# Sixteen 512-byte stores of zeros to the last tile's rows, sent on ScalarE's queue with the first load

## The chip, the core and the metric

The kernel runs on one NeuronCore of a Trainium2 chip. The metric is device time in microseconds (us) of one execution; the span that the profile shows is some 1.7 us shorter.

## The reference

```python
def reference(x, factor):            # x: 16 x 3 x 512 x 512 float32, factor 1.5
    mean = np.mean(x, axis=(2, 3), keepdims=True)
    return np.clip(mean + factor * (x - mean), 0, 1).astype(np.float32)
```

50.33 MB come in and 50.33 MB go out. There are 48 images; a tile of 128 partitions by 8192 elements (4.19 MB) holds four of them, so there are 12 tiles.

## The kernel before

Six tile buffers are loaded ahead on SyncE's queue (q1 in the profile). For each tile, VectorE sums one half of the columns and ScalarE the other, TensorE turns the sums into a bias, ScalarE applies scale, bias and Relu, and VectorE the upper bound. The tile's store goes out on ScalarE's queue (q10), and a buffer is loaded again when its store has landed.

```python
P = 128; ROW = 8192; BUFS = 6; CHUNK = 2048
...
    def load(t):
        xt = xpool.tile([P, ROW], f32, name="xt")
        nc.sync.dma_start(out=xt, in_=dram(x_f, t))
        tiles[t] = xt
...
    def store(t):
        nc.scalar.dma_start(out=dram(out_f, t), in_=tiles.pop(t))

    with tc.manual_schedule():
        for t in range(min(BUFS, n_tiles)):
            load(t)
        for t in range(n_tiles):
            compute(t)
            store(t)
            if t + BUFS < n_tiles:
                load(t + BUFS)
```

## Time and profile before

| | before |
|---|---|
| time, 3 runs | 240.37 us median (240.15 to 240.40) |
| span in the profile | 238.7 us |
| ScalarE, VectorE, TensorE busy | 60%, 47%, 7% |
| bytes moved | 100.66 MB: 232 us at 434 GB/s |

From the page of the kernel before: the DMA row (busy share of the 16 DMA engines in tenths, in 40 equal slices of the span), the GB/s row of the same slices, the two queues, and the DMA issues (KB each, median us from issue to landing).

```profile
span 238.7 us, 429 instructions
...
DMA  7999999999999999999999999999999999999995
GB/s 264 439 439 439 439 351 439 439 439 412 428 434 439 434 434 434 424 439 434 412 423 439 439 439 434 434 439 434 434 430 434 434 439 434 401 439 439 434 439 220
...
q1 hardware_dynamic: 1728, 50.33, 49.5%
q10 hardware_dynamic: 1728, 50.33, 49.0%
...
xt<-in_x_dram SPq DMA_DIRECT2D x12, 4096.0 KB, 58.1
out_dram<-xt ACTq DMA_DIRECT2D x12, 4096.0 KB, 36.3
```

The DMA engines are full from the second slice to the last but one, at about 434 GB/s. A slice is 6 us, and a packet's bytes are counted where it starts, so single steps of 5 to 30 GB/s mean little. The sixth slice, "slice 5" counted from 0, does mean something: 351 GB/s, between 29.8 and 35.8 us. The timeline of the kernel before tells what happens then (start, duration, engine, what):

```profile
0.75 2.96 SPq L65 DMA_DIRECT2D xt<-in_x_dram  x6
...
13.10 4.42 DVE L72 TENSOR_REDUCE sums<-xt 128x1 f32<-128x4096 f32 x1 [13.10 <-DMA xt<-in_x_dram]
...
28.28 0.37 ACTq L92 DMA_DIRECT2D out_dram<-xt  x1
```

The first store is issued at 28.28 us, just ahead of the slow slice. The trace also holds one record for each DMA packet. Chained by their starts and ends, they give what each DMA engine did. Four of the 16 chains, before (L: a 32 KB load packet, S: a 32 KB store packet, L4 and S4: a load's or a store's 4-byte completion write; start in ns from the span's start, then +duration):

```
L@28116+1213 L@29325+1213 L@30535+1776 S@32308+1213 L4@33517+9 S@33523+1213
L@27752+1213 L@28962+1213 L@30171+2052 L4@32219+9 L@32225+1492 S@33713+1213
L@28155+1213 L@29364+1458 L@30818+1993 S@32808+1213 L4@34017+9 S@34023+1213
L@28222+1213 L@29431+1213 L@30641+1945 L4@32582+9 L@32588+1391 S@33975+1213
```

A packet takes 1213 ns, on and on. Just ahead of the first store packet, one or two load packets on each engine take up to 2220 ns. The store packets themselves take 1213, but for one of 1260 (in a chain not shown).

I turn these records into lost time: each packet's bytes are spread evenly over its duration, and a stretch loses its length minus its bytes over 433.5 GB/s, the steady rate. By this measure the kernel before loses 0.85 us between 28 and 36 us, and 2.70 us in the first 4 us (of which 1.74 pass before the first packet).

### The profile page before, as it was taken

How to read it: one execution, taken by the hardware profiler on the slowest of the kernel's cores; microseconds unless marked ns; L12 is line 12 of the kernel's file. 1: busy time of each engine (PE TensorE's matmuls, PEld its weight loads, DVE VectorE, ACT ScalarE, POOL GpSimd, SP SyncE). 2: the span in 40 equal slices, each digit the busy share in tenths (PEclk: the TensorE clock that was granted, in tenths of full speed). 3: DMA queues.
4: the chain of work that ended last, by engine and by line, in shares of the span. 5: the costliest groups of instructions: out<-in, count | busy, mean ns of one | idle time of the engine just before them, and what ended most of it. 6: DMA issues, size and time to landing. Idle time of an engine off the chain costs nothing.

```text
span 238.7 us, 429 instructions
## 1 busy us (share of the span) xinstructions
PE 17.2 (7%) x72; PEld 16.3 (7%) x72; DVE 111.6 (47%) x60; ACT 143.4 (60%) x109; POOL 0.9 (0%) x9
## 2 busy tenths in 40 slices
PE   0001020020200200200200200020020020010000
PEld 0001020020200200200200200020020020010000
DVE  0073746927469254362562744725436255274400
ACT  2067779777797754681791693676468169169300
POOL 1000000000000000000000000000000000000000
DMA  7999999999999999999999999999999999999995
GB/s 264 439 439 439 439 351 439 439 439 412 428 434 439 434 434 434 424 439 434 412 423 439 439 439 434 434 439 434 434 430 434 434 439 434 401 439 439 434 439 220
DMA packets 3458, 100.68 MB, mean 422 GB/s; under 512 B 384, under 2 KB 384, under 8 KB 384
## 3 DMA queue, kind: packets, MB, share of 16 engines
q1 hardware_dynamic: 1728, 50.33, 49.5%
q10 hardware_dynamic: 1728, 50.33, 49.0%
q14 instruction: 2, 0.02, 0.0%
HBM read 50.33 MB, written 50.33 MB: 422 GB/s over the span
## 4 chain that ended last, share of the span: by engine, by line
ACT 38%; DVE 27%; another core or an unknown queue 13%; PE 7%; DMA 5%; issue 3%; DVEq 0%
ACT xt L88 37%; DVE sums L72 22%; PE pbias L83 7%; DMA xt<-in_x_dram 5%; DVE xt L89 5%; ACT bias L85 1%; DVEq L72 0%
## 5 line engine op out<-in xcount | busy, mean ns | idle before, releaser
L88 ACT ACTIVATE xt<-xt,bias 128x2048 f32<-128x2048 f32 x48 | 92.1, 1990 | 0.4
L89 DVE TENSOR_SCALAR xt<-xt 128x2048 f32<-128x2048 f32 x48 | 58.9, 1227 | 69.1 <-ACT xt L88 69.1
L78 ACT ACTIVATE junk<-xt 128x2048 f32<-128x2048 f32 x24 | 45.8, 1910 | 58.3 <-DMA xt<-in_x_dram 51.2
L72 DVE TENSOR_REDUCE sums<-xt 128x1 f32<-128x4096 f32 x12 | 53.0, 4418 | 43.6 <-DMA xt<-in_x_dram 43.6
L83 PE MATMUL pbias<-sums,blockw 128*128 128x1 f32 x72 | 17.2, 355 | 197.9 <-DVE sums L72 197.9
L83 PEld LDWEIGHTS pbias<-sums,blockw 128*128 128x128 f32 x72 | 16.3, 326 | 198.8 <-DVE sums L72 181.2
L85 ACT COPY bias<-pbias 128x1 f32<-128x1 f32 x12 | 1.9, 159 | 20.2 <-PE pbias L83 20.2
L78 ACT ACTIVATION_READ_ACCUMULATOR junk<-xt 128x1 f32 x24 | 4.5, 186 | 0.0
L78 ACT ACT_TABLE_LOAD x1 | 1.3, 1283 | 0.7 <-PEq L118 0.7
L59 POOL MEMSET blockw<- 32x32 f32 x4 | 0.5, 117 | 0.2
L57 POOL MEMSET blockw<- 128x128 f32 x1 | 0.2, 204 | 0.3 <-POOLq L118 0.3
L118 POOL MEMSET const-bfloat16-1.0<- 128x1 bf16 x1 | 0.1, 112 | 0.0
L118 POOL MEMSET const-uint8-127<- 128x1 uint8 x1 | 0.1, 112 | 0.0
L118 POOL MEMSET const-float32-1.0<- 128x1 f32 x1 | 0.1, 108 | 0.0
L118 POOL MEMSET const-float32-0.0<- 128x1 f32 x1 | 0.1, 103 | 0.2 <-issue 0.2
## 6 DMA issues: line engine op xcount, KB each, us to landing
xt<-in_x_dram SPq DMA_DIRECT2D x12, 4096.0 KB, 58.1
out_dram<-xt ACTq DMA_DIRECT2D x12, 4096.0 KB, 36.3
```

The lines of the kernel that those rows point to most:

```text
L57: nc.gpsimd.memset(blockw, 0.0)
L59: nc.gpsimd.memset(blockw[a : a + ppi, a : a + ppi], wconst)
L72: nc.vector.tensor_reduce(out=sums[:, 0:1], in_=xt[:, 0:HALF], axis=mybir.AxisListType.X, op=Alu.add)
L78: nc.scalar.activation(out=junk, in_=xt[:, a : a + JUNK], func=Act.Copy, accum_out=sums[:, 1 + j : 2 + j])
L83: nc.tensor.matmul(pbias, blockw, sums[:, j : j + 1], start=j == 0, stop=j == n_act)
L85: nc.scalar.copy(out=bias, in_=pbias)
L88: nc.scalar.activation(out=part, in_=part, func=Act.Relu, bias=bias, scale=factor)
L89: nc.vector.tensor_scalar(out=part, in0=part, scalar1=1.0, scalar2=None, op0=Alu.min)
L118: nc = _bacc.Bacc("TRN2", target_bir_lowering=False, num_devices=1)
```

## The change

The intent is to pay beforehand, while the first load starts up, whatever ScalarE's queue pays on its first use. The early store is tiny: 16 rows of 512 B, one for each DMA engine. It goes to rows of the last tile, which the last store writes again.

```diff
+    zeros = consts.tile([16, 128], f32, name="zeros")
+    nc.vector.memset(zeros, 0.0)
+    last = (n_tiles - 1) * P * ROW
+    early = bass.AP(tensor=out_f.tensor, offset=last, ap=[[8 * ROW, 16], [1, 128]])
 ...
     with tc.manual_schedule():
+        nc.scalar.dma_start(out=early, in_=zeros)
         for t in range(min(BUFS, n_tiles)):
             load(t)
```

## The prediction

> **What bounds the kernel now.** Data movement. The page's DMA queues show 50.33 MB in and 50.33 MB out; the DMA row is 9 in every slice but the first and the last, at 434 to 439 GB/s in most slices. 100.66 MB at 434 GB/s takes 232 of the span's 238.7 us. ScalarE (60%) and VectorE (47%) are not the limit. The last store is issued at 224.4 us (timeline) and the span ends at 238.7, so about 4 us of the previous store were still queued: the compute that the chain of waits follows has slack. Time can only come from where the DMA engines run below 434 GB/s: the opening (264 GB/s in slice 0), the end, and slice 5 (351 GB/s, 29.8 to 35.8 us). Slice 5 is where the first store starts (issued on ScalarE's queue at 28.3 us, timeline).
>
> **The cost aimed at.** In the trace's packet records, a 32 KB packet takes 1.213 us. The packets in flight about 2.3 to 4 us after the first store's issue took 1.56 to 2.22 us on all 16 engines, and these are load packets; the store's own packets, right behind, took 1.21. In sum 0.82 us lost per engine (0.85 from the rate). No later store shows it. The first packets of the first load, 1.0 us after its issue, are stretched alike (1.97 us on average, 0.76 lost). I read it as a one-time cost of a queue's first use.
>
> **What the change does.** It adds a 16x128 memset on VectorE (estimate 0.1 us; a 128x128 one on GpSimd took 0.20), one DMA issue on ScalarE (0.37 us for the first store) ahead of its table load, and 16 packets of 512 B, one on each engine. ("DMA: Bandwidth & Descriptors" of the Trainium skill, section "Why a DMA increments its semaphore by 16", says that 16 outermost rows are spread over 16 engines.) ScalarE is idle until the first load lands at 13.1 us: none of that is on the path. By the order of instructions the semaphores rotate by one place: the sixth load now waits for the first. Four loads of some 9.7 us are still queued then, so this should cost nothing.
>
> ScalarE's queue is first used at about 1 us instead of 28.3. The dip in slice 5 should go. What does the opening pay? The same page, section "Issuing engines are not separate DMA queues", says that both queues run on the same 16 engines and interleave; the trace agrees (store and load packets alternate). So the two first-use stalls may overlap (gain about 0.8 us) or follow one another, hitting the first load's second packets (gain near 0). The early store is issued some 0.2 us after the first load, so I expect mostly overlap: 0.1 to 0.4 us longer.
>
> **Prediction.** 240.37 - 0.85 + 0.2 = 239.7 us; range 239.2 to 240.5. Within 2%: 0.98; faster 0.01, slower 0.01.
>
> **What would show it.** Right: slice 5 at 434 to 439 GB/s; load packets near the first big store stay at 1.21 us; the first reduce starts at 13.1 to 13.5 us; the sixth load's issue moves to about 13 us without a DMA gap. Wrong: slice 5 still near 350 GB/s (the cost belongs to the first large store or to new output addresses, not to the queue), or the first reduce starts 0.8 us later (the stalls add up).
>
> **What would make it wrong.** A stall tied to the loads in flight or the store's size; small writes delaying the first load beyond 0.5 us; a gap from the later sixth load.

## The result

| | before | after |
|---|---|---|
| time, 4 runs each | 240.26 us median (239.67 to 240.40) | 240.07 us median (239.98 to 240.35) |
| ratio after / before | | 0.9999, 95% interval 0.998 to 1.0018 |
| span in the profile | 238.7 us | 238.3 us |
| lost in the first 4 us | 2.70 us | 2.68 us |
| lost at the first full store, 28 to 36 us | 0.85 us | 1.20 us |
| first reduce starts | 13.10 us | 12.98 us |

A ratio is the mean time of one kernel's fast runs over the mean of the other's of the same rounds, so it is not quite the ratio of the medians quoted.

The same lines of the page, after:

```profile
span 238.3 us, 431 instructions
...
GB/s 264 441 440 440 440 336 440 435 435 435 429 429 418 429 440 430 440 440 418 435 440 440 440 429 424 424 435 435 435 436 435 424 435 440 440 435 429 424 435 259
...
q10 hardware_dynamic: 1760, 50.34, 49.0%
...
out_dram<-zeros ACTq DMA_DIRECT2D x1, 8.0 KB, 7.1
```

The early store is there: 32 more packets on q10, 16 of data and 16 completion writes. It landed 7.1 us after its issue. Slice 0 is as before, at 264 GB/s, so the opening pays nothing for it. But slice 5 is not repaired: 336 GB/s, against 351 before. The timeline, after:

```profile
0.75 12.56 SPq L71 DMA_DIRECT2D xt<-in_x_dram  x6
0.83 0.17 DVE L63 MEMSET zeros<- 16x128 f32 x1 [0.83 <-PEq L125]
...
1.02 0.42 ACTq L101 DMA_DIRECT2D out_dram<-zeros  x1
...
12.98 4.42 DVE L78 TENSOR_REDUCE sums<-xt 128x1 f32<-128x4096 f32 x1 [11.99 <-DMA xt<-in_x_dram]
...
28.16 0.36 ACTq L98 DMA_DIRECT2D out_dram<-xt  x1
```

The memset took 0.17 us and the issue 0.42, both far from the critical path. The six load issues now span 12.56 us instead of 2.96, as the sixth waits for the first load; four loads were queued, and no gap opened. Four DMA engines' chains at the first full store, after:

```
L@28158+1213 L@29367+1276 L@30640+1871 S@32507+1213 L4@33717+9 S@33722+1213
L@28035+1213 L@29245+1568 L@31072+1833 S@32901+1213 L4@34111+9 S@34117+1213
L@28133+1213 L@29343+1213 L@30552+2599 L4@33147+9 L@33153+1213 S@34362+1213
L@28379+1213 L@29588+1213 L@30798+2885 L4@33679+9 L@33685+1213 S@34894+1213
```

The stretched load packets stand where they stood. The queue had been used and the cost was not paid. The loss is 0.35 us higher than before, and the highest at any unpaid first store: the others below lost 0.80 to 1.02 us. The three other runs with small early stores lost 0.87 to 0.98, so one profile does not show that the small stores raised it.

### The profile page after: what moved, and what is told of

It reads as the page before. It is cut to its first block, busy times and chain, and to the rows that moved or that the text cites. A ratio compares the mean times of both kernels' runs of the same rounds, so it can differ in the third digit from the quotient of the medians.

```text
span 238.3 us, 431 instructions
## 1 busy us (share of the span) xinstructions
PE 17.3 (7%) x72; PEld 16.3 (7%) x72; DVE 111.8 (47%) x61; ACT 143.4 (60%) x109; POOL 0.9 (0%) x9
## 4 chain that ended last, share of the span: by engine, by line
ACT 38%; DVE 27%; another core or an unknown queue 13%; PE 7%; DMA 5%; issue 3%; DVEq 0%
ACT xt L94 37%; DVE sums L78 22%; PE pbias L89 7%; DVE xt L95 5%; DMA xt<-in_x_dram 5%; ACT bias L91 1%; DVEq L78 0%
```

## The experiments

The dip is read from each run's trace. It is worth at most half a per cent, and the kernel before itself measured 239.65 to 240.03 us in the single runs beside these, so the times of single runs prove nothing about it. Each run below was timed and profiled once. All runs were correct. (The expectations worked with a rate of 434 GB/s, which makes some losses 0.01 us higher than in the text and the tables.)

### What kind of first use is it?

**More descriptors: 128 rows of 512 B.**

```diff
-    zeros = consts.tile([16, 128], f32, name="zeros")
-    early = ... ap=[[8 * ROW, 16], [1, 128]])
+    zeros = consts.tile([P, 128], f32, name="zeros")
+    early = ... ap=[[ROW, P], [1, 128]])
```

> The early store goes to 128 rows of 512 B instead of 16: 8 packets for each DMA engine instead of 1, as many as a full store has. After the change, the first large store still cost 1.20 us of DMA time between 28 and 40 us (before: 0.85). Theory COUNT (the cost is the ScalarE queue's first burst of many descriptors): the loss between 28 and 40 us falls below 0.2 us. Theories BYTES, WRITES and START (the cost is tied to the amount, to the first large write to the output, or to the start of any large store on an idle queue): it stays at 0.8 to 1.2 us.

Measured: 0.97 us lost at 28 to 36 us. Eight small packets per engine prepay no more than one; COUNT falls. They ran from 6.0 to 14.1 us, so it is not that small packets went out only while the first load started up. (240.75 us; the kernel before beside it 239.79.)

**More bytes: 128 rows of 7168 B.**

```diff
-    zeros = consts.tile([16, 128], f32, name="zeros")
-    early = ... ap=[[8 * ROW, 16], [1, 128]])
+    zeros = consts.tile([P, 1792], f32, name="zeros")
+    early = ... ap=[[ROW, P], [1, 1792]])
```

> The early store is 128 rows of 7168 B, 0.92 MB (about 2.1 us of DMA time at 434 GB/s, so the time should rise by about 2 us). Theory QUEUE or WRITES (a one-time cost of the first large transfer on this queue, or of the first large write): the loss between 28 and 40 us falls below 0.2 us, and packets of 1.5 us and more appear near the early store. Theory START (each start of a large store on an idle queue, beside a streaming load queue): it stays at 0.8 to 1.2 us.

Measured: 0.37 us at 28 to 36 us, so less, but not gone. Near the early store, some load packets were stretched to about 1.3 to 1.5 us: 0.32 us lost between 4 and 20 us, against 0.05 before. 241.78 us, beside 239.79. Neither theory as I put it: part of the cost had moved to the early store. What matters is thus something in which 7 KB packets come nearer to the full store than 512-byte packets do.

**The queue without a store: the second load on ScalarE's queue.** No early store; against the kernel before:

```diff
-        nc.sync.dma_start(out=xt, in_=dram(x_f, t))
+        (nc.scalar if t == 1 else nc.sync).dma_start(out=xt, in_=dram(x_f, t))
```

> No early store; the second load goes out on ScalarE's queue, so that queue is first used by a full 4 MB transfer at 0.75 us, without any write to the output. Theory QUEUE (first large use of that queue, in any direction): no loss beyond 0.2 us when the first store starts (some 8 us later than before, as the first two loads share the engines). Theory WRITES (first large write) or START: 0.8 to 1.2 us are still lost within 5 us of the first store's issue.

Measured: the first store is issued at 37.7 us, and 1.02 us are lost between 37 and 45 us. ScalarE's queue had moved a whole 4 MB load before that, with no stretch of its own (2.57 us lost in the first 4 us, no more than before). The GB/s row of this run's page has its low slice at the first store, one slice later than before:

```profile
GB/s 269 434 439 439 439 439 362 423 439 423 439 439 434 428 439 406 428 430 428 439 439 434 439 439 439 439 428 435 423 412 434 434 428 434 439 439 439 439 434 203
```

So it is not the queue's first use that costs. It is storing. 240.45 us, beside 239.79.

**The first store later.** Against the kernel before, the first store is placed after the second tile's work:

```diff
             compute(t)
+            if t == 0:
+                continue
+            if t == 1:
+                store(0)
+                load(BUFS)
             store(t)
```

> No early store; the first store is issued after the second tile's work, at about 43 us instead of 28 us. If the dip belongs to the store, it moves with it: packets over 1.5 us at 45 to 48 us and none at 29 to 33 us, 0.8 to 1.2 us lost. If it belongs to the loads or to the time since the start (rival PLACE), it stays at 29 to 33 us.

Measured: the store was issued at 34.1 us, not 43 (in the trace it goes out at the start of the first of four activations that stand before it in the source; why is not shown). The dip went with it: 0.85 us lost between 33 and 41 us, the long packets start at 35 to 39 us, none at 29 to 33. PLACE falls. The page's row, with slice 6 low instead of slice 5:

```profile
GB/s 270 436 441 441 441 441 347 441 441 441 436 436 414 425 414 442 441 436 441 441 436 436 436 425 419 414 441 441 437 436 441 436 430 441 425 419 419 441 441 265
```

This run took 239.49 us, beside 239.79; one run, within the spread of the kernel before, so no gain is claimed.

### Once, or at every start? And does the address matter?

**A pause in the stores.**

```diff
             compute(t)
+            if t in (1, 2):
+                continue
+            if t == 3:
+                for held in (1, 2):
+                    store(held)
+                    load(held + BUFS)
             store(t)
```

> The second and third stores are held until the fourth tile's work is done, so that after the first store has drained (about 52 us) only loads run for some 10 us, and then large stores start again (issue at about 64 us). Theory ONCE (a one-time cost of the first large write of the program): 0.8 to 1.2 us lost at 28 to 34 us, under 0.2 us at the restart. Theory START (each change from loads alone to loads and large stores): 0.8 to 1.2 us lost at both places, in load packets of 1.5 to 2.9 us right ahead of the store's first packet.

Measured: 0.80 us lost at 28 to 36 us, and 0.01 us at the restart (64 to 72 us), though only loads had run from 52 to 68 us. Two windows of this run, at the first store and at the restart (stretch and its length in us, busy us of TensorE's matmuls and weight loads, VectorE, ScalarE and GpSimd, clock, DMA share, and GB/s as the last number):

```profile
28.00:34.00 6.00, 1.39 (x6) 1.35 (x6) 4.55 (x2) 4.01 (x4) 0.00 (x0) 1.00 1.03 388
64.00:70.00 6.00, 0.03 (x1) 0.00 (x0) 2.46 (x2) 5.90 (x5) 0.00 (x0) 1.00 0.99 426
```

388 is the dip; 426 is a whole stretch (steady ones of this length count 415 to 438, by where packets happen to start). In the packet records no 32 KB packet that starts between 62 and 72 us takes over 1364 ns. So the cost did not come back after the pause; START falls. 239.69 us, beside 239.80.

**Four early stores of 0.92 MB**, against the run with one:

```diff
-    early = bass.AP(tensor=out_f.tensor, offset=last, ap=[[ROW, P], [1, 1792]])
+    early = [
+        bass.AP(tensor=out_f.tensor, offset=last + k * 1792, ap=[[ROW, P], [1, 1792]])
+        for k in range(4)
+    ]
...
-        nc.scalar.dma_start(out=early, in_=zeros)
+        for e in early:
+            nc.scalar.dma_start(out=e, in_=zeros)
```

> Four early stores of 0.92 MB to the last tile's rows, 3.67 MB in all, done at about 20 us (8.5 us more DMA time, so about 249 us). One early store of this kind had cut the loss at the first full store from about 1.0 to 0.38 us, with some 0.3 us lost near the early store instead. Theory BILL (a fixed amount of loss that the first megabytes written pay off): under 0.1 us at the first full store, 0.6 us or more between 4 and 20 us. Theory START (what is lost belongs to each start of large store packets behind loads): 0.4 to 1.2 us at the first full store, no less than with one early store.

Measured: these stores did not end at 20 us. A 7 KB store packet and a 32 KB load packet take turns on each engine, so the last of each engine's 32 small packets came at about 53 us. 0.38 us were lost between 4 and 20 us. When 32 KB store packets then followed, without a pause, 0.25 us were lost again (50 to 58 us), in load packets of about 1.3 to 1.5 us on all 16 engines. 248.24 us, beside 239.80. BILL wanted under 0.1: megabytes written do not settle the account while the packets are small.

**The first tile's store in four parts of 8 KB rows**, against the kernel before (`store(0)` is left out):

```diff
             nc.vector.tensor_scalar(out=part, in0=part, scalar1=1.0, scalar2=None, op0=Alu.min)
+            if t == 0:
+                o = bass.AP(tensor=out_f.tensor, offset=c, ap=[[ROW, P], [1, CHUNK]])
+                nc.scalar.dma_start(out=o, in_=part)
```

> No early store; the first tile's output goes out in four column parts of 1 MB (8 KB rows), each as soon as it is done, from about 22.6 us on. Theory START: one loss when the first part starts, at 24 to 28 us, smaller the smaller the store's packets are (8 KB instead of 32 KB: 0.3 to 0.5 us), and under 0.1 us for later parts that follow without a pause. Theory BILL: 0.8 to 1.2 us in all, over the parts.

Measured: 0.07 us at 24 to 28 us, and 0.23 us at 30 to 34 us when the second part was under way. The first full-size store started while no load was in flight, as the small packets had held up the first store, and with it the next load, until 71 us. Then 0.28 us were lost when the loads came back (74 to 80 us), and 0.83 us where the third tile's store began (83 to 91 us), in load packets of up to 2.1 us. The first part is cheaper than START expected (0.3 to 0.5 us), and neither theory foretold the late loss. By then each engine had stored eight 32 KB packets, from 70.7 us on, the first four or five of them with no load in flight. So this run does not fit the account that the other runs give, and no run here tells why the loss came at the second full-size store and not at the first. 240.55 us, beside 239.80. Inconclusive.

**Sixteen early rows in the first tile.**

```diff
-    last = (n_tiles - 1) * P * ROW
+    last = 0
```

> The change as it is, but the sixteen early 512-byte stores go to the first tile's rows (16 of those that the first full store writes). Theory ADDRESS (the loss is a first touch of the output's addresses near the first tile): it falls below 0.3 us at the first full store. All other theories: it stays at 0.8 to 1.2 us.

Measured: 0.98 us lost at 28 to 36 us. 239.90 us, beside 239.80.

**All 128 rows of the first tile**, so that each DMA engine touches the rows that it will write:

```diff
-    last = (n_tiles - 1) * P * ROW
-    early = ... ap=[[8 * ROW, 16], [1, 128]])
+    last = 0
+    early = ... ap=[[ROW, P], [1, 128]])
```

> The early store writes 512 B at the head of each of the first tile's 128 rows, so each DMA engine touches beforehand the very rows that it writes in the first full store. Theory ADDRESS (each engine pays for its first touch of the addresses): the loss at the first full store falls below 0.3 us. Theories PACKET and BYTES (small packets leave the cost unpaid): it stays at 0.8 to 1.2 us, as with 128 rows of the last tile (0.98).

Measured: 0.87 us lost at 28 to 36 us; 239.77 us, beside 239.65. With the run before it and the change itself, ADDRESS falls: 512-byte stores prepay nothing, whether they touch the last tile's rows or the first tile's own.

### Full-size packets

**One 32 KB packet for each engine.** A source row of 32 KB needs room, so one tile buffer goes.

```diff
-BUFS = 6
+BUFS = 5
-    zeros = consts.tile([16, 128], f32, name="zeros")
-    early = ... ap=[[8 * ROW, 16], [1, 128]])
+    zeros = consts.tile([16, ROW], f32, name="zeros")
+    early = ... ap=[[8 * ROW, 16], [1, ROW]])
```

> Five tile buffers instead of six (for room), and the early store is 16 rows of 32 KB: one full-size packet for each DMA engine, 0.52 MB in all (1.2 us more DMA time), issued at about 9 us after a long memset. Theory PACKET (each engine's first full-size store packet is what costs, once): the stretch of load packets (1.5 us and more, 0.6 to 1.2 us in all) appears at 11 to 15 us, ahead of the early packets, and under 0.2 us is left at the first full store. Theory BYTES (the cost is worked off by some megabytes of stores): 0.1 to 0.3 us at the early store and 0.4 to 1.0 us left at the first full store.

Measured: at the first full store, nothing is lost at all. Every 32 KB packet that starts between 28 and 36 us takes 1213 ns, loads and stores. The early packets had ended at about 17 us, 15 us before the first full store's packets began. Four chains of this run at the first full store:

```
L@28439+1213 L@29648+1213 L@30858+1213 L@32067+1213 S@33276+1213 L@34486+1213
L@28752+1213 L@29961+1213 L@31171+1213 S@32380+1213 L@33589+1213 S@34799+1213
L@28561+1213 L@29771+1213 L@30980+1213 S@32189+1213 L@33399+1213 S@34608+1213
L@29164+1213 L@30373+1213 L@31582+1213 S@32792+1213 L@34001+1213 S@35211+1213
```

The page's row of this run has slice 5 whole, and the loss in slice 2, at the early store:

```profile
GB/s 261 435 332 435 435 435 435 435 429 435 435 435 435 429 435 435 420 435 429 435 435 429 424 435 435 435 435 435 435 436 429 435 429 435 429 435 435 342 435 261
```

What was paid was more than what was saved. PACKET is right about the first full store, but it had expected long load packets ahead of the early store; here it was the early store packets themselves that were long (2.1 to 3.3 us), and 1.75 us were lost between 9 and 20 us. BYTES falls: the run with 7 KB packets had stored more on each engine (57 KB in eight packets, from 6.2 to 17.5 us) and had still lost 0.37 us, whereas one 32 KB packet, at 13.4 to 16.9 us, left nothing. The low slice near the end (342) is something else: the DMA engines ran out of work before the last store was issued at 229.1 us, and 1.65 us were lost at 226 to 232 us. The 4 us of queued stores that the kernel before has at that point were used up. The run took 242.97 us, beside 239.65.

**The control: five buffers, no early store**, against the kernel before:

```diff
-BUFS = 6
+BUFS = 5
```

> Control for the run with one 32 KB packet per engine: five tile buffers, no early store. Theory PACKET: without the early packets the loss at the first full store is back, 0.8 to 1.2 us between 28 and 34 us. Rival BUFFERS (it was the fifth buffer's absence that removed it): under 0.2 us.

Measured: 0.81 us at 28 to 36 us, so it is not the missing buffer that cured it. 239.91 us, beside 240.03: the sixth buffer buys nothing that one run can show. The window from 28 to 34 us of the two runs, first with the early packets, then without (GB/s is the last number):

```profile
28.00:34.00 6.00, 1.30 (x6) 1.30 (x6) 4.65 (x2) 4.01 (x4) 0.00 (x0) 1.00 1.00 431
```

```profile
28.00:34.00 6.00, 1.31 (x6) 1.31 (x6) 4.64 (x2) 4.00 (x4) 0.00 (x0) 1.00 1.05 393
```

**A full early store**, against the run with one packet per engine:

```diff
-    zeros = consts.tile([16, ROW], f32, name="zeros")
-    early = ... ap=[[8 * ROW, 16], [1, ROW]])
+    zeros = consts.tile([P, ROW], f32, name="zeros")
+    early = ... ap=[[ROW, P], [1, ROW]])
```

> Five buffers, and the early store is a full tile of zeros (128 rows of 32 KB, 4.19 MB, 9.7 us more DMA time), issued at about 9 us, as like the first full store as can be. In the run with one packet per engine those packets took 2.2 to 3.3 us each (1.65 us lost per engine), which rival PORTS puts down to 16 engines reading from 16 neighbouring partitions. Theory PACKET with PORTS: here the loads ahead of the early store are stretched as at a first full store (0.8 to 1.2 us lost at 10 to 16 us), the early packets take 1.21 us, and under 0.2 us is lost at the first full store. Without PORTS: the early store's first packets take over 2 us again.

Measured: 0.70 us were lost at 9 to 17 us (a little under the 0.8 to 1.2 expected), in load packets of up to 1.92 us just ahead of the early store's first packets, which took 1213 ns; the first full store lost 0.03 us. The dip has moved, from the store of the first tile to the store of zeros (here the one followed the other without a pause). The time was 256.23 us, beside 240.03: 16.2 us more. The 4.19 MB explain 9.7 of it; most of the rest is at the end again, where by the packet records no data moves from 236.4 to 243.3 us, until the last store, issued at 242.4 us, begins.

The difference from the run before speaks for PORTS. "SBUF — State Buffer" of the Trainium skill, section "Door 1: The DMA port swizzle", gives a map by which 16 neighbouring partitions reach only 4 of the 16 DMA ports. The runs agree in direction: 2.1 to 3.3 us a packet from 16 neighbouring partitions, 1.21 us from all 128. It is not the factor of four that this map alone would give, and the two runs differ in more than that.

### Summary

| run | early store | lost at the first full store |
|---|---|---|
| before | none | 0.85 us |
| after (the change) | 16 rows of 512 B, last tile | 1.20 us |
| 128 rows of 512 B | last tile | 0.97 us |
| 16 rows of 512 B | first tile | 0.98 us |
| 128 rows of 512 B | first tile | 0.87 us |
| second load on ScalarE's queue | none | 1.02 us |
| first store later | none | 0.85 us |
| pause in the stores | none | 0.80 us, and 0.01 at the restart |
| first store in four parts of 8 KB rows | none | 0.07 and 0.23 us at the parts, 0.83 at the second full-size store |
| 128 rows of 7168 B | last tile | 0.37 us |
| four times 128 rows of 7168 B | last tile | 0.25 us |
| five buffers | none | 0.81 us |
| five buffers | 16 rows of 32 KB | 0.00 us |
| five buffers | 128 rows of 32 KB | 0.03 us, without a pause before it |

What is shown, the run with four parts apart: the loss moves with the first store made of large packets; it did not come back after a pause; packets of 512 B leave it unpaid, whether there are one or eight on each engine, and in both places that they wrote to; packets of 7 KB pay a part; after one 32 KB packet on each engine nothing of it is left. That rests on one profile for each, against nine of unpaid first stores with 0.80 to 1.20 us. What stays open: what in the hardware it is, why the run with four parts lost 0.83 us so late, after full-size packets, and whether the similar stretch of the first load packets (1.97 us on average) is the same thing on the load side. That the second load's queue paid none of its own in the second-load run fits this, but was not tested further.

No version beat the kernel before. Of the sizes tried, only full-size packets prepaid the whole loss, and one such packet on each engine costs 1.2 us of DMA time by itself, more than the 0.85 us that the kernel before loses. In the runs made, the early store was stretched as well. An early store of 16 KB packets at the very start was not tried.

A rival that no run set by itself: that the loss comes when the engines' packets start nearly together, and that any earlier stretch, once it has spread their starts, takes it away. The packet records let us look. Just before the first full store, the starts of the 16 engines' load packets, taken as places within one packet time of 1.21 us, lay within 0.34 to 0.85 us in the runs that lost 0.80 us or more, and within 1.02 us in the run with one 32 KB packet per engine. But the change and the run with 7 KB packets had the same spread (0.46 and 0.48 us) and lost 1.20 and 0.37, and at the restart after the pause the spread was 0.75 us and the loss 0.01. So this spread alone does not decide; that it has a part in the loss is not excluded.

## Why the prediction was right in its number and wrong in its reason

- **The bound** (data movement, 434 GB/s from end to end) was right; the rate outside the opening, the first store and the end is the same after.
- **The place and size of the dip** (0.85 us at the first store, on all 16 engines, in load packets) was right; all profiles with an unpaid first store gave 0.80 to 1.20.
- **"I read it as a one-time cost of a queue's first use"** is the step that failed. "One-time" was right: a pause of some 15 us in the stores did not bring it back. "Of a queue's first use" was wrong: the early store used the queue, and so did a whole 4 MB load, and the dip stayed (1.20 and 1.02 us). In its place the runs showed that it goes with the first store of large packets: after one 32 KB store packet on each engine, 0.00 us were lost, against 0.81 in the same kernel without them. The prediction had named this among the signs of being wrong ("the cost belongs to the first large store"), but gave it no weight in the number.
- **"The dip in slice 5 should go"** (-0.85 us): it did not; 336 GB/s after, 351 before.
- **The opening's price** (+0.1 to 0.4 us): zero, 2.68 against 2.70 us, and the first reduce started 0.12 us earlier. As the early store did not meet the cost, it had nothing to hand over to the opening.
- **Memset, issue, and the sixth load's new wait** costing nothing: right (0.17 and 0.42 us on idle engines; the sixth load issued at about 13 us without a gap).
- **The number**: 239.7 us foretold, 240.07 measured, ratio 0.9999 against the 0.997 that 239.7 over 240.37 stands for. The measured time lies within 239.2 to 240.5 because the range made room for no gain. Of the two terms of the sum, the saving of 0.85 did not come and the price of 0.2 was not paid; that the result lay within the range is luck as far as the reason goes.

## What to carry to other kernels

A start-up cost can be prepaid only by work of the kind that incurs it: find out what counts (here the size of the store's packets, not the queue, the address or the number of descriptors) before building a cheap stand-in for it. On a resource that is full from end to end, expect a gain from prepaying only if the payment falls into time in which that resource is idle, or costs less than what it saves; here it did neither (1.75 us lost at the early 32 KB packets, about 0.8 saved later). When a change leaves the time alone, look whether the dip that it aimed at is still in the trace: an unchanged time within the foretold range does not mean that the reason was right.

## What the Trainium skill lacked or had wrong

- "DMA: Bandwidth & Descriptors" does not tell of a one-time loss at a program's first large stores: 0.80 to 1.20 us of all 16 engines' time in the profiles where nothing had prepaid it, none after one 32 KB store packet on each engine. (One run, with its first store in four parts, lost 0.83 us after full-size packets.)
- The same page, section "Latency and other measured facts", gives about 600 ns to the first byte for DMAs from SyncE and ScalarE. The first load's first packet came 1.0 us after its issue began on idle engines, but behind a streaming load queue the first full store's first packet came 4.0 us after its issue began (28.28 to 32.3 us), and the early 8 KB store's 5.1 us after (1.02 to 6.11 us).
- The same page, section "Where 436 GB/s comes from", says that for transfers between HBM and SBUF the HBM side (about 358 GB/s) binds, though its own figure for a 16 MB load on one core (425 GB/s) lies above that. One core moved 434 GB/s here, loads and stores together, for more than 200 us: above the figure for the HBM side and close to the page's figure for the fabric (435).
- The same page, section "Queues, rings and completion order", says that an engine switches between queues at packets of about 9 to 17 descriptors. The records here show single 32 KB packets, one row each, of the two queues taking turns; a small packet gets one turn for each large one, so a 0.92 MB store in 7 KB packets held its queue for about 11 us (6.2 to 17.5 us).
